# Four late matrix blocks of a decoder layer: another order of the sums, of the loads and of two products

## The chip, the core and the metric

The kernel runs on one core of one Trainium2 chip. TensorE (PE) multiplies matrices into PSUM, VectorE (DVE), ScalarE (ACT) and GpSimd (POOL) work element by element, and 16 DMA engines move data between HBM and SBUF. DMAs are issued from the queues of SyncE (SP), ScalarE and GpSimd. Each engine executes its own instructions in program order and waits on semaphores for the others. The metric is the device time of one execution in microseconds; the time of a kernel is the median of its runs.

## What is computed

The reference is one layer of a hybrid decoder over 512 tokens of width 2048 in float32. The part that the change touches is its end:

```python
merged = g_a * (o_a @ w_up_a[l]) + g_b * (o_b @ w_up_b[l])
x = x + merged @ w_out[l]
x = x + jax.nn.sigmoid(x @ w_ple_gate[l]) * (p[l] @ w_ple[l])
return rms_norm(x, final_g)
```

`w_out` and `w_ple_gate` are 2048 x 2048. What comes before (the projection of 2048 to 10800 columns, sparse attention, the gated spatial mixer and the two products up to `merged`) is the same in both kernels.

## The kernel before

**Accuracy.** A float32 operand is split into a high part, rounded by a cast on ScalarE (`high`, line 180), and a low part, the difference, on VectorE (`low`, line 186). Each product is then three matmuls (lines 443 to 445): high by high, high activations by low weights, low activations by high weights.

**Seven products instead of eight.** Each of the two matrix products at the end is done in a scheme of the Strassen kind. The 512 tokens are cut in two halves of 256 (two token tiles of 128 each), the 2048 contracted rows in two halves of 1024, and the 2048 columns in blocks. There are four such jobs, called the late blocks, in this order: `wo0` and `wo1` (for `w_out`), then `pg1` and `pg0` (for `w_ple_gate`). A block makes 1024 output columns, 512 of the left and 512 of the right half of the matrix, in seven products, named 1, 5, 6, 3, 7, 2 and 4. Each product has four pieces, 0 to 3, of 256 rows, so a block has 28 pieces; a piece is 12 matmuls of 128 x 512. Pieces are written as product and number: 70 is the first piece of product 7. The order is that of `LATE` (line 79): for wo0 and pg1

`10 11 12 13 20 21 50 51 22 23 52 53 60 30 61 31 62 32 63 33 70 71 72 73 40 41 42 43`

and for wo1 and pg0 the same with 52 53 before 22 23, and 60 61 62 63 before 30 31 32 33. "Piece 19" or "step 19" of a block below is the place in this order, counted from 0: in all four, places 20 to 23 are product 7 and places 24 to 27 product 4.

**PSUM.** A block has three pairs of banks (`BANK_OF`): products 1, 6, 7 and 4 accumulate one upon the other in the first pair, 5 and 3 in the second, 2 in the third. So each result has to be read out (`evac_late`) before the next product of the same pair starts. In `evac_late` products 1, 5 and 6 are copied by ScalarE (line 924); 3, 7 and 2 are combined on VectorE with an earlier copy straight out of PSUM (lines 930 and 932); 4 is the last.

**Weights of a block.** The first and second halves of the rows and of the columns give quarters 11, 12, 21 and 22, each in four tiles of 256 rows x 512 columns (512 KB). Operands of products are made in place: product 1 uses 11, 5 uses 11 + 12, 6 uses 11 + 12 + 22, 4 uses 11 + 12 + 22 + 21; product 2 uses 21, 3 uses 22, 7 uses 22 + 12. A sum is made either by a DMA that accumulates into the tile, issued by GpSimd (`add_later`, line 345), or on VectorE from a loaded tile (line 327, in `sum_to`). `adds` says which: "6" in `adds` means that 22 is accumulated by DMA for the first two pieces of product 6, "4" that 21 is accumulated by DMA for product 4. Without "4" the tiles of 21 are loaded a second time ("21b") and added on VectorE. The addition of 12 is always a DMA. Before the change wo0 and pg1 have "6", wo1 and pg0 have "4".

**Loads.** All loads of weights are issued by SP in the order of the list `loads` (`load_next`, `load_to`, line 291). Tiles of 11 have four places ("more"), all others five ("late": three named raw and two named ext). A load is put into the program once the last piece that read its place has been split; `held_till` puts a load later: not before the given piece has been split.

**Order of the instructions.** `gemm` writes the program piece by piece. At each step it first runs what was put off (`flush`, list `deferred`; `later` puts off by two steps), then `split_to`: the cast and the low part of the piece two further on, with sums, `add_later` and loads; then what `plan` and `plan_steps` have put at this step; then the 12 matmuls; after the last piece of a product its read-out. The buffers of high and low parts (`hs`, `ls`) have three places each, so a cast can be at most two pieces ahead of TensorE. An engine that waits on one of these instructions holds up all that were written after it for the same engine.

**Activations.** The operands of the next block's products are made beside the running block: eight transposes into two banks (`turn_pair`, line 2026), then sums on VectorE and casts on ScalarE (`first_half`, `second_half`). They are four sets, A, B, C and E, each a list of steps (A0, A1, ...), and a text in `plan_steps` says at which step of the block which of them stand. In `second_half`, 0 is the transposes with the high parts, 1 the first sum and low parts, and then follow casts of sums (ScalarE), their low parts and further sums (VectorE).

**End of a block.** Results of wo0 and wo1 are added to tiles of x (`add_x`, line 917), which `load_x` brings on ScalarE's queue. Those of pg1 and pg0 go through a tanh (`gate_x2`, line 956) and two operations of VectorE (949, 951). In pg0 product 4 is done token tile by token tile, and `finish_tile` scales and stores finished rows.

The loop over the token tiles in a piece, before:

```python
for i in range(2):
    k = 2 * j + i
    for t in range(2):
        o = sets[b][t]
        # three matmuls into o
if k == half - 1:
    job.evac(p, sets[b])
```

Of the kernel before, what the change touches and what calls it, by code (L numbers as in the profile page):

```python
# [102 lines left out]
def kernel(ctx: ExitStack, tc: tile.TileContext, x, p, norm_g, w_in,  # L103
                      pe_k, w1_k, w2_k, pe_v, w1_v, w2_v, ln_g, ln_b, sgu_w, sgu_b,
                      w_up_a, w_up_b, w_out, w_ple, w_ple_gate, final_g, out):
    nc = tc.nc
# [114 lines left out]
    def add_job(job):  # L221
        jobs.append(job)
        if job.kind == "S":
            half, c2 = job.kt // 2, job.c2
            ld = {}
            if job.grown:
# [120 lines left out]
    def split_to(i, more=1):  # L347
# [17 lines left out]
        while state["low"] <= min(i, len(subs) - 1):  # L365
# [16 lines left out]
            if job.grown and k == "7" and "4" in job.adds:  # L382
                add_later(job.grown, raw[ld["11", n]], "21", n)
# [11 lines left out]
    def gemm():  # L395
        si = 0
        for job in jobs:
            if job.kind == "S":
# [3 lines left out]
                for at, (p, j) in enumerate(products(job)):  # L402
# [33 lines left out]
                    for i in range(2):  # L436
                        k = 2 * j + i
                        st, sp = k == 0 and p in "152", k == half - 1
                        for t in range(2):
                            o = sets[b][t]  # L440
                            ah, al = job.act(p, k, t)
                            go = p not in "152"
                            nc.tensor.matmul(o, ah, hi[:, i], start=st, stop=False, skip_group_check=go)  # L443
                            nc.tensor.matmul(o, ah, lo[:, i], start=False, stop=False, skip_group_check=go)  # L444
                            nc.tensor.matmul(o, al, hi[:, i], start=False, stop=sp, skip_group_check=go)  # L445
                            if not (i and t):
                                yield
                    if k == half - 1:
                        job.evac(p, sets[b])
# [469 lines left out]
    def evac_late(i, final, fourth):  # L919

        def e(p, ps, t=None):
# [3 lines left out]
            elif p in "372":  # L925
                other, row, cg = {"3": ("6", 0, i + 2), "7": ("5", 2, i + 2), "2": ("1", 0, i)}[p]
# [15 lines left out]
    def final_wo(p, cg, row):  # L942
        other = {"3": "6", "7": "5", "2": "1"}[p]
        for t in range(2):
            if p != "2":
                later(partial(add_x, cg, row + t, kept[other][t]))
# [21 lines left out]
    def final_pg(p, cg, row):  # L968
        other = {"3": "6", "7": "5", "2": "1"}[p]
        for t in range(2):  # L970
# [1234 lines left out]
    plan_steps((late_jobs["wo0"], late_jobs["wo1"]), 0, "A0 A1B0 B1A2 C0A3 C1E0B2 E1B3 C2A4 C3E2A5 A6 E3A7 A8B4 B5C4 B6B7 B8C5 C6C7 C8E4 E5E6E7 E8", items)  # L2205
# [16 lines left out]
    plan_steps((late_jobs["wo1"], late_jobs["pg1"]), 9, "A0 A1 A2 A3B0 B1 B2 B3 C0 C1 C2E0 C3E1 E2 E3", items)  # L2222
    plan("wo1", 11, partial(load_x, 3, partial(new_gates, "x_3")))
    plan("wo1", 16, partial(load_x, 1, new_x))
# [87 lines left out]
```

## Time and profile before

| | |
|---|---|
| median of 3 runs | 1552.41 us (1551.02 to 1553.17) |
| profiled execution | 1551.73 us, span 1550.0 us |
| granted TensorE clock, mean | 0.989 |
| TensorE matmuls, busy | 1510.6 us (97%) |
| VectorE, busy | 1228.9 us (79%) |
| ScalarE, busy | 861.2 us (56%) |
| GpSimd, busy | 349.1 us (23%) |
| HBM read and written | 246.79 MB and 73.27 MB |

Busy time of TensorE counts modelled ends of pipelined matmuls, so gaps are read from the starts. A row of a timeline is: start, duration, engine, line, operation, what it writes and reads, shape, count; in brackets the idle time of the engine before it and what ended that. A row of waits is: engine, tile, line, what it waited for, then microseconds in total, times and the longest. A row of windows is: the stretch, its length, busy time and count of TensorE's matmuls, its weight loads, VectorE, ScalarE and GpSimd, then the granted clock, the share of the DMA engines and GB/s. A row "DMA tile<-source" of the chain is the time from issue to landing on which the chain waited; a row of DMA issues is queue, operation, count, size and the median time from issue to landing.

### The profile page before, as it was taken

What the parts mean: (1) busy time and instruction counts of PE and PEld (TensorE: products, weight loads), DVE (VectorE), ACT (ScalarE), POOL (GpSimd) and SP (SyncE); (2) the same over time, 40 slices, a digit from 0 to 9 for tenths busy, and PEclk for the clock granted to TensorE, in tenths of its full rate; (3) what the DMA queues carried; (4) which work ended last, traced back from release to release, by engine and by line L of the source; (5) the groups of instructions that cost most, each with busy time, mean ns of one, the idle gap of its engine ahead of it and who ended that gap; (6) DMA issues with size and microseconds to landing.
All of it is one profiled execution on the core that took longest, in us unless ns stands there. A gap on an engine that the chain in (4) does not pass through costs nothing.

```text
span 1550.0 us, 20203 instructions
## 1 busy us (share of the span) xinstructions
PE 1510.6 (97%) x7174; PEld 1255.2 (81%) x7174; DVE 1228.9 (79%) x1798; ACT 861.2 (56%) x1431; POOL 349.1 (23%) x495
## 2 busy tenths in 40 slices
PE   9999999999999999999999999999999999999995
PEld 8988888888888888888888888887888777777774
DVE  7787877777889787878588898859989976688576
ACT  6454455444555555555577776755556434455446
POOL 2232334220121111113214333321122110211120
PEclk9999999999999999999999999999999999999997
DMA  9897969582548585779634454377898776985875
GB/s 323 217 305 187 259 110 287 162 252 89 198 148 254 176 265 180 228 252 287 148 85 108 106 111 106 88 276 251 276 241 205 163 203 178 212 195 122 231 195 157
DMA packets 197076, 303.56 MB, mean 196 GB/s; under 512 B 30264, under 2 KB 91360, under 8 KB 195568
## 3 DMA queue, kind: packets, MB, share of 16 engines
q0 software_dynamic: 77856, 120.98, 33.6%
q1 hardware_dynamic: 104912, 149.57, 30.4%
q10 hardware_dynamic: 14208, 31.72, 6.0%
q8 instruction: 56, 0.92, 0.2%
q14 instruction: 44, 0.36, 0.1%
HBM read 246.79 MB, written 73.27 MB: 206 GB/s over the span
## 4 chain that ended last, share of the span: by engine, by line
PE 82%; DVE 6%; DMA 4%; ACT 4%; issue 3%; POOL 1%; ACTq 0%; DVEq 0%; POOLq 0%
PE ps_m L445 7%; PE ps_m L443 7%; PE ps_m L444 7%; DMA more<-in_w_out_dram 2%; DVE ls L186 2%; PE ps_pg L444 2%; PE ps_t L1710 2%; PE ps_pg L445 2%; PE ps_pg L443 2%; PE ps_za L474 2%; PE ps_za L473 2%; PE ps_za L472 2%; PE ps_u L443 2%; PE ps_kv L443 2%; PE ps_zb L443 2%
## 5 line engine op out<-in xcount | busy, mean ns | idle before, releaser
L186 DVE TENSOR_TENSOR ls<-b,hs 128x1024 fp32r<-128x1024 f32 x160 | 195.7, 1223 | 100.9 <-ACT hs L180 100.1
L180 ACT CAST hs<-b 128x1024 fp32r<-128x1024 f32 x160 | 168.1, 1052 | 189.9 <-PE ps_m L445 64.2
L180 ACT CAST hs<-raw 128x1024 fp32r<-128x1024 f32 x118 | 124.2, 1053 | 135.1 <-PE ps_m L445 28.9
L186 DVE TENSOR_TENSOR ls<-raw,hs 128x1024 fp32r<-128x1024 f32 x118 | 144.1, 1222 | 48.9 <-ACT hs L180 48.9
L180 ACT CAST hs<-more 128x1024 fp32r<-128x1024 f32 x95 | 99.9, 1052 | 117.8 <-DVE more L327 21.7
L186 DVE TENSOR_TENSOR ls<-more,hs 128x1024 fp32r<-128x1024 f32 x95 | 115.9, 1221 | 59.1 <-ACT hs L180 58.7
L443 PE MATMUL ps_m<-hs,act_h 128*128 128x512 f32 x256 | 100.2, 391 | 0.0
L445 PE MATMUL ps_m<-hs,act_l 128*128 128x512 f32 x256 | 99.6, 389 | 0.0
L444 PE MATMUL ps_m<-ls,act_h 128*128 128x512 f32 x256 | 99.6, 389 | 0.0
L186 DVE TENSOR_TENSOR lo<-raw,hi 128x512 fp32r<-128x512 f32 (+1 forms) x96 | 63.9, 670 | 19.9 <-PE ps_za L474 7.6
L332 DVE TENSOR_TENSOR b<-b,b 128x1024 f32<-128x1024 f32 x64 | 78.0, 1219 | 0.1
L332 DVE TENSOR_TENSOR b<-raw,b 128x1024 f32<-128x1024 f32 x64 | 77.9, 1218 | 0.0
L1659 ACT ACTIVATE prob<-prob,st 128x512 f32<-128x512 f32 (+3 forms) x128 | 70.8, 560 | 5.7 <-DVE st L1650 5.7
L1650 DVE CUSTOM_DVE_ANT_0 prob<-ps_s,b 128x512 f32<-128x512 f32 (+3 forms) x128 | 56.3, 486 | 13.7 <-PE ps_s L1646 13.5
L180 ACT CAST pth<-ps_t 128x512 fp32r<-128x512 f32 (+1 forms) x88 | 44.1, 547 | 35.0 <-PE ps_t L1710 34.5
L180 ACT CAST hi<-raw 128x512 fp32r<-128x512 f32 (+1 forms) x94 | 54.2, 588 | 15.9 <-PE ps_kw L473 4.0
L445 PEld LDWEIGHTS ps_m<-hs,act_l 128*128 128x128 f32 x256 | 48.1, 188 | 10.0
L444 PEld LDWEIGHTS ps_m<-ls,act_h 128*128 128x128 f32 x256 | 48.1, 188 | 9.8
L443 PEld LDWEIGHTS ps_m<-hs,act_h 128*128 128x128 f32 x256 | 48.1, 188 | 9.8
L186 DVE TENSOR_TENSOR ptl<-ps_t,pth 128x512 fp32r<-128x512 f32 (+1 forms) x88 | 52.4, 633 | 3.4 <-ACT pth L180 3.4
L443 PE MATMUL ps_wo<-hs,m_h 128*128 128x512 f32 x128 | 51.1, 399 | 2.3 <-DVE keep L932 1.3
L444 PE MATMUL ps_wo<-ls,m_h 128*128 128x512 f32 x128 | 50.8, 397 | 1.8 <-DVE ls L186 1.8
(661 smaller groups left out, 4566.3 us busy)
## 6 DMA issues: line engine op xcount, KB each, us to landing
raw<-in_w_in_dram SPq DMA_DIRECT2D x100, 512.0 KB, 4.4
b<-in_w_in_dram SPq DMA_DIRECT2D x64, 512.0 KB, 5.8
more<-in_w_out_dram POOLq DMA_DIRECT2D x14, 512.0 KB, 10.6
more<-in_w_ple_gate_dram POOLq DMA_DIRECT2D x14, 512.0 KB, 11.5
gate<-keep ACTq DMA_DIRECT2D x24, 256.0 KB, 6.4
raw<-in_w_up_b_dram SPq DMA_DIRECT2D x12, 512.0 KB, 7.4
raw<-in_w_up_a_dram SPq DMA_DIRECT2D x12, 512.0 KB, 5.6
raw<-in_w_out_dram SPq DMA_DIRECT2D x12, 512.0 KB, 9.9
```

Of the source, the lines that this page charges most:

```text
L180: nc.scalar.copy(hi, src)
L186: nc.vector.tensor_tensor(out=lo, in0=src, in1=hi.bitcast(F32), op=ALU.subtract)
L332: nc.vector.tensor_tensor(out=b[o], in0=b[x], in1=b[y], op=ALU.subtract)
L443: nc.tensor.matmul(o, ah, hi[:, i], start=st, stop=False, skip_group_check=go)
L444: nc.tensor.matmul(o, ah, lo[:, i], start=False, stop=False, skip_group_check=go)
L445: nc.tensor.matmul(o, al, hi[:, i], start=False, stop=sp, skip_group_check=go)
L472: nc.tensor.matmul(ps, hi[:, j], ah, start=st, stop=False)
L473: nc.tensor.matmul(ps, hi[:, j], al, start=False, stop=False)
L474: nc.tensor.matmul(ps, lo[:, j], ah, start=False, stop=sp)
L1650: nc.vector.tensor_tensor_reduce(out=pt[:, j * n:j * n + n], in0=o[:, j], in1=b0[:, 512 - n:], scale=-SLOPE[h], scalar=3.0e38, op0=ALU.add ...
L1659: nc.scalar.activation(sl, sl, AF.Exp, bias=st[:, 0, j, hh:hh + 1], scale=-1.0, accum_out=st[:, 1, j, hh:hh + 1])
L1710: nc.tensor.transpose(b[:, (2 * e + hh) * P:(2 * e + hh + 1) * P], pts[hh][:, c:c + P], ident)
```

## The change

It does six things, all in the late blocks:

- Products 7 and 4 do their pieces token tile by token tile: the six matmuls of tile 0, then the six of tile 1. Product 7 is read out per token tile: ScalarE copies it to `kept["6"]` as soon as that tile's last matmul has been written into the program, half-way through piece 73 for tile 0, and the subtraction on VectorE is put off to the next step.
- The texts of `plan_steps` place casts of sums on ScalarE one step after the sum on VectorE that they read, and the low part in the step of its cast; most steps of sets stand earlier than before. B in pg1 turns into bank "t" instead of "s".
- `adds` is "64" for wo0, "4" for wo1, "64" for pg1 and nothing for pg0. So wo0 and pg1 accumulate 21 by DMA, and pg0 loads 21b and adds on VectorE.
- Before each DMA that accumulates 21, GpSimd copies one element of the tile of 22, so that it waits for what was accumulated into that tile.
- The load of the third tile of 21 is held in the program until piece 3 of its block has been split.
- `load_x`, `add_x`, `load_x2` and `load_fg` (the broadcast of `final_g`, 1 MB) stand at other steps.

```diff
@@ add_job
                 if first:
                     held_till.update({ld["21", 3]: len(subs) + 4, ld["22", 0]: len(subs) + 7})
+                held_till[ld["21", 2]] = len(subs) + 3
@@ split_to
             if job.grown and k == "7" and "4" in job.adds:
+                nc.gpsimd.tensor_copy(small[0:1, 76:77], raw[ld["22", n]][0:1, 0, 0:1])
                 add_later(job.grown, raw[ld["11", n]], "21", n)
@@ gemm
-                    for i in range(2):
+                    turned = job.grown and p in "74"
+                    for n in range(4):
+                        t, i = divmod(n, 2) if turned else (n % 2, n // 2)
...
+                        if turned and sp and p == "7":
+                            job.evac(p, sets[b], t)
+                        if n < 3:
+                            yield
-                    if k == half - 1:
+                    if k == half - 1 and not (turned and p == "7"):
                         job.evac(p, sets[b])
@@ evac_late
+            elif p == "7":
+                nc.scalar.copy(kept["6"][t], ps[t])
+
+                def difference(o=kept["5"][t], x=kept["6"][t], t=t):
+                    nc.vector.scalar_tensor_tensor(out=o, in0=x, scalar=-1.0, in1=o, op0=ALU.mult, op1=ALU.subtract)
+                    final(p, i + 2, 2, (t,))
+                deferred.append(difference)
@@ final_wo
-                later(partial(add_x, cg, row + t, kept[other][t]))
+                (deferred.append if p == "7" else later)(partial(add_x, cg, row + t, kept[other][t]))
@@ final_pg
-                (deferred.append if cg % 2 == 0 else later)(f)
+                (deferred.append if cg % 2 == 0 or p == "7" else later)(f)
@@ late_jobs
-                                       seq=LATE[at], adds="64"[at])
+                                       seq=LATE[at], adds={"wo0": "64", "wo1": "4", "pg1": "64", "pg0": ""}[f"{n}{i}"])
@@ plans, wo0
-"A0 A1B0 B1A2 C0A3 C1E0B2 E1B3 C2A4 C3E2A5 A6 E3A7 A8B4 B5C4 B6B7 B8C5 C6C7 C8E4 E5E6E7 E8"
+"A0 A1B0 B1A2A3 C0B2B3 C1E0 E1C2C3 E2E3A4 A5A6 A7A8B4 B5B6 B7B8C4 C5C6 C7C8E4 E5E6 E7E8"
-    plan("wo0", 19, partial(load_x, 0, new_x))
-    for n, at in (("wo0", 24), ("wo1", 25)):
+    plan("wo0", 21, partial(load_x, 0, new_x))
+    for n, at in (("wo0", 26), ("wo1", 26)):
@@ plans, wo1 from step 9
-"A0 A1 A2 A3B0 B1 B2 B3 C0 C1 C2E0 C3E1 E2 E3"
-    plan("wo1", 11, partial(load_x, 3, partial(new_gates, "x_3")))
-    plan("wo1", 16, partial(load_x, 1, new_x))
+"A0 A1 A2A3 B0 B1 B2B3 - C0 C1 C2C3E0 E1 E2E3"
+    plan("wo1", 14, partial(load_x, 3, partial(new_gates, "x_3")))
+    plan("wo1", 21, partial(load_x, 1, new_x))
@@ plans, wo1 from step 25 and pg1 (banks of A, B, C, E first)
-("gg", "ss", "gg", "oo")
-"A0 A1B0 B1A2 A3 A4B2 B3C0 B4C1E0 E1 A5C2 C3E2A6 E3A7B5 B6 B7 C4 C5C6 C7 C8 E4 E5E6 E7 E8"
+("gg", "tt", "gg", "oo")
+"A0 A1B0 B1A2 A3A4 B2 C0B3B4 C1E0A5 E1C2C3 E2E3A6A7 C4B5 C5C6B6B7 C7C8 E4 E5E6 E7E8"
@@ plans, pg0
-    plan("pg0", 9, partial(load_x2, 0, "h2"))
-    plan("pg0", 11, partial(load_x2, 2, "h1"))
+    plan("pg0", 8, partial(load_x2, 0, "h2"))
+    plan("pg0", 10, partial(load_x2, 2, "h1"))
-    plan("pg0", 15, load_fg)
+    plan("pg0", 14, load_fg)
```

More of the change, by code (lines that the diff above doesn't have):

```diff
@@ L435, in gemm @@
                         sets[b] = [bank(job.banks[b], f"ps_{job.name}{b}{t}") for t in range(2)]
-                    for i in range(2):
+                    turned = job.grown and p in "74"
+                    for n in range(4):
+                        t, i = divmod(n, 2) if turned else (n % 2, n // 2)
                         k = 2 * j + i
                         st, sp = k == 0 and p in "152", k == half - 1
[L439 to L447, printed above, removed]
-                    if k == half - 1:
+                        o = sets[b][t]
+                        ah, al = job.act(p, k, t)
+                        go = p not in "152"
+                        nc.tensor.matmul(o, ah, hi[:, i], start=st, stop=False, skip_group_check=go)
+                        nc.tensor.matmul(o, ah, lo[:, i], start=False, stop=False, skip_group_check=go)
+                        nc.tensor.matmul(o, al, hi[:, i], start=False, stop=sp, skip_group_check=go)
+                        if turned and sp and p == "7":
[3 more added lines that the diff above has]
+                    if k == half - 1 and not (turned and p == "7"):
                         job.evac(p, sets[b])
@@ L924, in e @@
                     nc.scalar.copy(kept[p][t], ps[t])
-            elif p in "372":
-                other, row, cg = {"3": ("6", 0, i + 2), "7": ("5", 2, i + 2), "2": ("1", 0, i)}[p]
+            elif p == "7":
[4 more added lines that the diff above has]
+                deferred.append(difference)
+            elif p in "32":
+                other, row, cg = {"3": ("6", 0, i + 2), "2": ("1", 0, i)}[p]
                 for t in range(2):
@@ L940, in evac_late, with final_wo @@
         return e
-    def final_wo(p, cg, row):
+    def final_wo(p, cg, row, ts=(0, 1)):
         other = {"3": "6", "7": "5", "2": "1"}[p]
-        for t in range(2):
+        for t in ts:
             if p != "2":
-                later(partial(add_x, cg, row + t, kept[other][t]))
+                (deferred.append if p == "7" else later)(partial(add_x, cg, row + t, kept[other][t]))
     def ple_add(cg, t, sg, piece):
@@ L966, in gate_x2, with final_pg @@
         (deferred.append if soon else later)(second)
-    def final_pg(p, cg, row):
+    def final_pg(p, cg, row, ts=(0, 1)):
         other = {"3": "6", "7": "5", "2": "1"}[p]
-        for t in range(2):
+        for t in ts:
             o = kept[other][t]
@@ L2204 @@
     plan("wo0", 5, lambda: sums_at.update(x=new_x()))
-    plan_steps((late_jobs["wo0"], late_jobs["wo1"]), 0, "A0 A1B0 B1A2 C0A3 C1E0B2 E1B3 C2A4 C3E2A5 A6 E3A7 A8B4 B5C4 B6B7 B8C5 C6C7 C8E4 E5E6E7 E8", items)
+    plan_steps((late_jobs["wo0"], late_jobs["wo1"]), 0, "A0 A1B0 B1A2A3 C0B2B3 C1E0 E1C2C3 E2E3A4 A5A6 A7A8B4 B5B6 B7B8C4 C5C6 C7C8E4 E5E6 E7E8", items)
     plan("wo0", 8, partial(load_x, 2, partial(new_gates, "x_2")))
-    plan("wo0", 19, partial(load_x, 0, new_x))
-    for n, at in (("wo0", 24), ("wo1", 25)):
+    plan("wo0", 21, partial(load_x, 0, new_x))
+    for n, at in (("wo0", 26), ("wo1", 26)):
         for t in range(2):
@@ L2221 @@
                                  partial(sums_tile, *third), ("gg", "gg", "gg", "tt")[n])
-    plan_steps((late_jobs["wo1"], late_jobs["pg1"]), 9, "A0 A1 A2 A3B0 B1 B2 B3 C0 C1 C2E0 C3E1 E2 E3", items)
-    plan("wo1", 11, partial(load_x, 3, partial(new_gates, "x_3")))
-    plan("wo1", 16, partial(load_x, 1, new_x))
+    plan_steps((late_jobs["wo1"], late_jobs["pg1"]), 9, "A0 A1 A2A3 B0 B1 B2B3 - C0 C1 C2C3E0 E1 E2E3", items)
+    plan("wo1", 14, partial(load_x, 3, partial(new_gates, "x_3")))
+    plan("wo1", 21, partial(load_x, 1, new_x))
     def second_places():
@@ L2240 @@
         items[name] = second_half(embedded, q, lambda cg=cg: x_tiles[cg], j, partial(sums_tile, *own),
-                                  partial(sums_tile, "6", 2), a21 and partial(sums_tile, *a21), ("gg", "ss", "gg", "oo")[n])
+                                  partial(sums_tile, "6", 2), a21 and partial(sums_tile, *a21), ("gg", "tt", "gg", "oo")[n])
     plan("wo1", 23, second_places)
     plan("pg1", 2, more_places)
-    plan_steps((late_jobs["wo1"], late_jobs["pg1"]), 25, "A0 A1B0 B1A2 A3 A4B2 B3C0 B4C1E0 E1 A5C2 C3E2A6 E3A7B5 "
-               "B6 B7 C4 C5C6 C7 C8 E4 E5E6 E7 E8", items)
+    plan_steps((late_jobs["wo1"], late_jobs["pg1"]), 25, "A0 A1B0 B1A2 A3A4 B2 C0B3B4 C1E0A5 E1C2C3 "
+               "E2E3A6A7 C4B5 C5C6B6B7 C7C8 E4 E5E6 E7E8", items)
     plan("pg1", 2, lambda: x2_tiles.update({1: x_tiles[1], 3: x_tiles[3]}))
```

## The prediction

> **What bounds the kernel now.** I read the page first (span, chain), then TensorE's matmuls in order of time around the four late blocks, then who ended TensorE's waits there, then VectorE's and the DMA engines' load.
>
> ```profile
> span 1550.0 us, 20203 instructions
> PE 82%; DVE 6%; DMA 4%; ACT 4%; issue 3%; POOL 1%; ACTq 0%; DVEq 0%; POOLq 0%
> ```
>
> The chain that ends last is TensorE's, and the diff touches only the last quarter. The blocks begin here (in this order wo0, wo1, pg1, pg0), and the last matmul is the sixth row. The seventh, from the chain, is one turn of eight transposes:
>
> ```profile
> 1183.32 0.48 PE L443 MATMUL ps_wo<-hs,m_h 128*128 128x512 f32 x1
> ...
> 1271.16 0.39 PE L443 MATMUL ps_wo<-hs,m_h 128*128 128x512 f32 x1
> 1271.38 0.39 PE L444 MATMUL ps_wo<-ls,m_h 128*128 128x512 f32 x1
> ...
> 1360.64 0.47 PE L443 MATMUL ps_pg<-hs,ob_h 128*128 128x512 f32 x1 [1.87 <-DVE s L186]
> ...
> 1448.76 0.39 PE L443 MATMUL ps_pg<-hs,ob_h 128*128 128x512 f32 x1
> ...
> 1536.38 0.39 PE L420 MATMUL ps_pg<-ob_h,m_l 128*128 128x512 f32 x1
> 1307.34 0.87 PE ps_m L2026 x8
> ```
>
> Undisturbed matmuls start 0.227 us apart, so a block of 28 pieces x 12 is 76.3 us and a piece 2.72. Less that and its transposes (0.9 for each turn inside it: three, six, two, none), wo0 (87.8 us) lost 8.8, wo1 (89.5) 7.7, pg1 (88.1) 10.0 and pg0 (88.0 to the end of its last matmul) 11.7: **38 us lost in all**. The change can win no more there. The losses of single pieces below are counted the same way, between their first matmuls. Who ended these waits:
>
> ```profile
> PE ps_pg L443 <- DVE keep L932: 4.9, 1, 4.9
> PE ps_wo L444 <- DVE ls L186: 4.9, 7, 1.0
> PE ps_pg L418 <- DVE keep L932: 3.5, 1, 3.5
> PE ps_pg L443 <- DVE s L186: 1.9, 1, 1.9
> PE ps_wo L443 <- DVE keep L932: 1.3, 2, 0.8
> ```
>
> L932 is the seventh product read out of PSUM, for which the fourth waits in the same bank; L186 is the low half of a weight piece. The rest is matmuls at half clock after such a wait, one row of it below.
>
> **The change part by part.**
>
> *Seventh product.* In pg1 its two read-outs stand on VectorE behind sums (L327) and low halves of later pieces:
>
> ```profile
> 1434.96 1.28 DVE L932 SCALAR_TENSOR_TENSOR keep<-ps_pg,keep 128x512 f32<-128x512 f32 x2
> 1435.79 0.77 PE L443 MATMUL ps_pg<-hs,s 128*128 128x512 f32 x1 [4.92 <-DVE keep L932]
> ```
>
> ```profile
> L924 ACT COPY keep<-ps_pg 128x512 f32<-128x512 f32 x12 | 7.0, 586 | 5.1 <-PE ps_pg L445 4.4 <-DVE x L186 0.2
> ```
>
> Now ScalarE copies a tile (0.59), issued half-way through piece 23 for token tile 0 (1.36 us before the piece ends), behind only the cast of piece 25. So copy 0 ends before piece 24, and copy 1 (0.6 after piece 23) within piece 24's first 1.36. What is late next is that cast: it waits for the accumulating DMA. A quiet one takes 6.3 us, as the row of 1396 to 1426 says; the last of four issued behind one another landed after 14.3:
>
> ```profile
> raw<-in_w_ple_gate_dram POOLq DMA_DIRECT2D x3, 512.0 KB, 6.3
> ...
> 1333.20 14.32 DMA more<-in_w_out_dram
> ```
>
> The four took 33.3% of 34 us of the DMA engines in the row of 1264 to 1298 below, 2.8 apiece; so the second "21" lands some 12 us after the low half of piece 19, 15 after piece 17's start, while the copy's end is wanted 19 after that start. Hidden, with 3 to spare after the cast. The subtraction moves to VectorE's next piece at the same 0.68. Won: in pg1 4.9 + 0.2 and 2.1 of half clock, 7.2, of which I take 6.9; in wo0 1.2, in wo1 0.6 (both in the items below).
>
> *wo0, pieces 22 to 24, 5.0 us.* The third copy of "22" lands late under three plain loads of "21b" beside it:
>
> ```profile
> 1241.65 10.85 DMA raw<-in_w_out_dram
> ```
>
> "4" among the additions removes these loads and four 1.14 us sums (in pg1 too), and puts four accumulations behind it. At 6.3 it lands before its cast is due. Gain 4.9 with the 1.2 above. The POOL copy of one element costs only its wait for "22"; behind it stand only later "21". Bound: nothing if the pieces come at 10.9 again, 5.0.
>
> *wo0, pieces 15 to 19, 3.9 us: VectorE is the limit.*
>
> ```profile
> 1193.00:1242.00 49.00, 47.13 (x207) 37.17 (x205) 44.66 (x61) 26.75 (x36) 6.32 (x6) 1.00 0.73 165
> ```
>
> Its 4.3 idle microseconds (3.8 of them waits for ScalarE) are all that the new order can take. I count the queue: the rows below give 0.67 for two of 256 columns, 1.19 for two of 512, 1.14 for a low half.
>
> ```profile
> 1190.28 0.75 DVE L2033 SCALAR_TENSOR_TENSOR keep<-ps_m,a 128x256 f32<-128x256 f32 x2
> 1190.95 1.28 DVE L188 SCALAR_TENSOR_TENSOR m_l<-ps_m,m_h 128x512 fp32r<-128x512 f32 x2
> 1192.14 1.21 DVE L186 TENSOR_TENSOR ls<-raw,hs 128x1024 fp32r<-128x1024 f32 x1
> ```
>
> A set (A, B, C or E) is 1.9 + 0.6 + 1.3 + 1.9 + 0.6 = 6.3 (a dependent pair 1.3 instead of 1.2). From 1192.14 to the end of piece 17's low half stand 14 low halves (16.0), A without its first part and three sets (23.5), two sums and two read-outs (3.5): 43.0, with 0.3 of waiting to 1235.4. TensorE undisturbed wants it at 1232.6. So 2.9 us stay of 3.9: the work is done sooner, but it also stands ahead of low halves sooner. Gain 1.0 (bounds -1 and 3.9).
>
> *wo1, pieces 8 and 9, 2.4 us:* casts wait for accumulations of the operand "12".
>
> ```profile
> 1276.68 19.97 DMA more<-in_w_out_dram
> ...
> q0 software_dynamic: 1088, 2.10, 33.3%
> q10 hardware_dynamic: 1056, 2.10, 16.0%
> ```
>
> ```profile
> 1266.94 0.42 SPq L291 DMA_DIRECT2D raw<-in_w_out_dram  x1
> 1267.42 0.97 SPq L291 DMA_DIRECT2D ext<-in_w_out_dram  x2
> 1268.49 11.02 SPq L291 DMA_DIRECT2D raw<-in_w_out_dram  x3
> ```
>
> The first five leave SP in a row because their places are free (the last row's third came 11 us later). Holding "21", 2 back moves its place in the program, but SP has only these loads in its queue, in the same order, and gets no new wait. I take the hold as nothing (bounds 0 and 2.4).
>
> *wo1, pieces 19 to 24, 3.3 us.* load_x of tile 1 stood before the transposes that still read its place, and ScalarE's casts stood behind it:
>
> ```profile
> 1326.36 0.92 ACTq L2165 DMA_DIRECT2D x<-in_x_dram  x2
> 1327.32 1.05 ACT L180 CAST hs<-ext 128x1024 fp32r<-128x1024 f32 x1 [5.19 <-PE ps_m L2026]
> ```
>
> At piece 21 those have run; its landing (5 to 6 us) is wanted at 26. Gain 2.8: 0.5 stays, since the turn at piece 25 needs the seventh's additions, which stand behind low half 26 and so behind a "21".
>
> *Begin of pg1 and its pieces 17 to 19, 5.0 us* (2.0 at 1360.64, 1.7 of half clock, 1.3). B's turned pair leaves bank "s" (pg1's first) for "t" (first needed at piece 4), so that wait goes. But VectorE is next:
>
> ```profile
> 1352.00:1379.00 27.00, 25.13 (x116) 20.54 (x116) 22.52 (x34) 14.64 (x21) 5.44 (x5) 0.94 0.93 233
> ```
>
> From wo1's piece 26 to pg1's low half 13 its queue holds 14 low halves (16.0), A and B (7.0 each), C and E (12.0), four additions (2.4), two read-outs (1.2): 45.6 against 15 pieces and three turns, 43.4. So 2.2 stay, gain 2.8 (bounds 0 and 5.0).
>
> *pg0* gives up "4": four loads and four 1.14 us sums return, where VectorE has no gap:
>
> ```profile
> 1515.24 1.22 DVE L186 TENSOR_TENSOR ls<-ext,hs 128x1024 fp32r<-128x1024 f32 x1
> ...
> 1517.58 2.35 DVE L186 TENSOR_TENSOR ls<-more,hs 128x1024 fp32r<-128x1024 f32 x2
> 1519.85 0.15 DVE L988 TENSOR_REDUCE small<-small 128x1 f32<-128x4 f32 x1
> ...
> 1521.99 1.28 DVE L932 SCALAR_TENSOR_TENSOR keep<-ps_pg,keep 128x512 f32<-128x512 f32 x2
> ```
>
> Three sums, 3.4 us, come ahead of L988. load_fg one piece earlier clears the way for "22", and low half 22 starts about 2.8 us sooner; L988 is then 0.6 later. ScalarE's copies of the seventh stand behind finish_tile(0), whose scalings end 0.6 later than their 1523.2, so the copy ends at 1524.4 where the first L932 ended at 1522.7:
>
> ```profile
> 1521.85 1.32 ACT L1004 ACTIVATE x<-x,small 128x512 f32<-128x512 f32 x2
> ...
> 1522.82 0.76 PE L418 MATMUL ps_pg<-hs,s 128*128 128x512 f32 x1 [3.50 <-DVE keep L932]
> 1523.38 0.63 PE L419 MATMUL ps_pg<-ls,s 128*128 128x512 f32 x1
> ```
>
> The fourth starts 1.5 later, the end, which ScalarE and VectorE carry from here, 1.2 later. Cost 1.2 (bounds: 4.3 if the "22" land no sooner, a gain of 3 if VectorE keeps up).
>
> *The rest at nothing.* Matmuls of products seven and four in the other order of token tiles are the same 12 to a piece with the same low half, which the piece has to have two matmuls in either way. load_x of tiles 3 and 0, add_x and load_x2 move by one to five pieces with the same instructions and transfers; what hides them is that their data is used four pieces later or more, and a lost cover would cost one landing, 5 to 8 us, once. The rows of additions on VectorE (L917) two pieces later meet pieces without sums.
>
> **Sum:** 6.9 + 4.9 + 1.0 + 0 + 2.8 + 2.8 - 1.2 = 17.2 us. The profiled execution took 1551.73 (span 1550.0), the median of the runs is 1552.41, 0.7 above it; 1552.4 - 17.2 = **1535.2 us**.
>
> The Trainium skill (TensorE: Matmul & The Clock Gate, Part 1: The HAM clock gate) lets the clock fall only after an idle window of about 3.4 us. The trace differs: a wait of 1.87 us at 1360.64 goes with a clock of 0.94 over 27 us, 1.6 us. By the rule alone the half clock at wo0 and at pg1's begin (3 us) would not hang on these waits, and the sum would be 14; the row decides.
>
> **The rivals.**
>
> *VectorE binds more than I count* (0.19). For it: 91% busy in wo0's stretch; against it: its idle time there. The two gains under it fall to 0 (-3.8) and pg0 costs 4.3 (-3.1): 10.3 won, 1542.
>
> *The waits go nearly all* (0.18): the hold acts (2.4), VectorE loses nothing in pg1 (2.2), and pg0 gains 2 instead of its cost (3.2). 25 won, 1527. Against it: the SP rows, and VectorE's queue.
>
> *Nothing won* (0.03): what is won in wo0 and pg1 is lost again behind late sums in pg0.
>
> *Slower* (0.10): one mechanism, accumulations too late. An accumulation takes twice the DMA time of a plain transfer (33.3% against 16.0% for 2.10 MB), and casts of the fourth's pieces wait for it with the seventh's copies behind them on ScalarE. If the "21" land in wo0, wo1 and pg1 as the last did at 1276 (20 us), the copy comes 5 us late with 2 of half clock in each: 21 lost against 17.2 won, 1556. It decides from a landing of 16 us on; for it speaks that row, against it the quiet 6.3. The Trainium skill (DMA: Bandwidth & Descriptors, Issuing engines are not separate DMA queues) says that all queues share 16 engines, which those shares agree with.
>
> **How the numbers follow.** Forecast 0.50, its own range 1530 to 1541. With the rivals the range is 1525 to 1547: it leaves out the last two and half of the better one's far side. About 0.2% (3 us) is what can be told from no change: faster 0.87, same 0.03, slower 0.10.
>
> **What would show it.** wo0 about 82 us from first to next first matmul, wo1 with pg1's begin about 84.5, pg1 about 80.5; no wait for L932 from the fourth's first matmul outside pg0; pg1's begin without a wait for s; no 5 us gap of ScalarE before L2165. SP's five loads still in a row at wo1's begin, and pieces 8 and 9 still late. In pg0 the fourth begins later in the block than now. I am wrong in place if wo0 or pg1 keep over 4 us of waits for low halves, in sign if the casts of the fourth's pieces wait for "21".

## The result, and the profile after

The changed kernel takes 1540.2 us (median of 4 runs, 1538.6 to 1540.4) against 1552.8 us (1551.0 to 1553.4) on the same chip: a ratio of 0.9918 with an interval of 0.9901 to 0.9936. It is faster by 12.6 us. The prediction was 1535.2 us, so 5.0 us are missing. The experiments show that its two largest terms can be won by other edits too than those it named, and that the cost in pg0 was put too low.

The page of the changed kernel has this span and this chain, and TensorE's timeline these first matmuls of the blocks and this last one:

```profile
span 1538.5 us, 20227 instructions
PE 83%; DVE 8%; ACT 3%; DMA 3%; issue 2%; POOL 0%; DVEq 0%; ACTq 0%; POOLq 0%
```

```profile
1183.55 0.48 PE L446 MATMUL ps_wo<-hs,m_h 128*128 128x512 f32 x1
...
1265.74 0.39 PE L446 MATMUL ps_wo<-hs,m_h 128*128 128x512 f32 x1
...
1351.45 0.39 PE L446 MATMUL ps_pg<-hs,ob_h 128*128 128x512 f32 x1
...
1433.21 0.39 PE L446 MATMUL ps_pg<-hs,ob_h 128*128 128x512 f32 x1
...
1524.50 0.39 PE L422 MATMUL ps_pg<-ob_h,m_l 128*128 128x512 f32 x1
```

The span is 11.5 us shorter. wo0 now takes 82.2 us (before 87.8), wo1 85.7 (89.5) and pg1 81.8 (88.1): 15.8 won. From the begin of pg0 to the end of the span it is 105.3 instead of 101.2: 4.1 lost. (The remaining 0.2 is the later begin of wo0.)

TensorE's three largest waits in the four blocks of the changed kernel, in total, times and the longest:

```profile
PE ps_pg L420 <- ACT keep L931: 5.1, 1, 5.1
PE ps_pg L447 <- DVE ls L186: 5.0, 4, 3.1
PE ps_wo L447 <- DVE ls L186: 2.9, 4, 1.2
```

The waits of 4.9 and 1.3 us for the seventh product (L932) and of 1.9 for bank "s" are gone. The first row is the seventh product again, now ScalarE's copy (L931), and it stands once, in pg0. In the list cut to pg1 alone no row names the seventh product.

The following table, worked out from each trace in the same way (first matmul of a block to that of the next, the last column from pg0's first matmul to the end of the span), carries the experiments. The kernels were timed on several chips, on which the kernel before took 1552.8 to 1554.1 us; each ratio is to the kernel before on the same chip, and medians some 1 us apart in different rows may differ by the chip alone:

| kernel | median, us | ratio to before (interval) | wo0 | wo1 | pg1 | pg0 and end |
|---|---|---|---|---|---|---|
| before | 1552.8 | | 87.8 | 89.5 | 88.1 | 101.2 |
| changed | 1540.2 | 0.9918 (0.9901 to 0.9936) | 82.2 | 85.7 | 81.8 | 105.3 |
| pg0_four | 1535.0 | 0.9884 (0.9869 to 0.9899) | 82.1 | 85.7 | 81.7 | 99.8 |
| finish_later | 1539.6 | 0.9915 (0.9900 to 0.9930) | 82.4 | 85.4 | 82.0 | 104.1 |
| no_four | 1541.5 | 0.9926 (0.9912 to 0.9941) | 82.1 | 85.8 | 83.6 | 105.7 |
| seventh_old | 1540.4 | 0.9917 (0.9900 to 0.9933) | 82.8 | 84.9 | 83.6 | 104.4 |
| both_back | 1544.8 | 0.9944 (0.9929 to 0.9959) | 82.8 | 85.9 | 87.3 | 103.5 |
| order_only | 1547.1 | 0.9967 (0.9955 to 0.9979) | 82.8 | 86.5 | 89.2 | 103.5 |
| old_order | 1544.1 | 0.9941 (0.9926 to 0.9956) | 85.2 | 88.5 | 80.3 | 104.5 |
| old_far_loads | 1542.4 | 0.9930 (0.9914 to 0.9945) | 83.6 | 87.4 | 81.7 | 104.8 |
| no_hold | 1538.8 | 0.9916 (0.9901 to 0.9931) | 82.2 | 85.1 | 81.8 | 105.0 |
| held_by_queue | 1531.9 | 0.9860 (0.9843 to 0.9876) | 82.1 | 83.1 | 81.9 | 99.5 |
| finish_25 | 1531.9 | 0.9872 (0.9855 to 0.9888) | 82.2 | 83.3 | 81.9 | 99.0 |
| finish_25_order | 1534.0 | 0.9883 (0.9868 to 0.9897) | 82.1 | 82.8 | 82.1 | 102.1 |

### The profile page after: what moved, and what is told of

It is laid out like the page before. It is cut to its first block, busy times and chain, and to the rows that moved or that the text cites. A ratio compares the mean times of both kernels' runs of the same rounds, so it can differ in the third digit from the quotient of the medians.

```text
span 1538.5 us, 20227 instructions
## 1 busy us (share of the span) xinstructions
PE 1502.8 (98%) x7174; PEld 1251.8 (81%) x7174; DVE 1225.2 (80%) x1794; ACT 865.2 (56%) x1439; POOL 355.6 (23%) x511
## 4 chain that ended last, share of the span: by engine, by line
PE 83%; DVE 8%; ACT 3%; DMA 3%; issue 2%; POOL 0%; DVEq 0%; ACTq 0%; POOLq 0%
PE ps_m L446 7%; PE ps_m L447 7%; PE ps_m L448 7%; DVE ls L186 2%; PE ps_wo L447 2%; PE ps_wo L448 2%; PE ps_wo L446 2%; PE ps_t L1722 2%; PE ps_za L479 2%; PE ps_za L478 2%; PE ps_za L477 2%; PE ps_u L446 2%; PE ps_zb L446 2%; PE ps_kv L446 2%; PE ps_vn L446 2%
## 5 line engine op out<-in xcount | busy, mean ns | idle before, releaser
L180 ACT CAST hs<-more 128x1024 fp32r<-128x1024 f32 x95 | 99.8, 1052 | 108.4 <-DVE more L328 26.7
L477 PE MATMUL ps_za<-act_h,hi 128*128 128x512 f32 x128 | 52.4, 409 | 0.0
L477 PE MATMUL ps_q<-act_h,hi 128*128 128x512 f32 x128 | 52.2, 407 | 0.0
## 6 DMA issues: line engine op xcount, KB each, us to landing
more<-in_w_out_dram POOLq DMA_DIRECT2D x18, 512.0 KB, 10.9
```

The source lines that it names most:

```text
L180: nc.scalar.copy(hi, src)
L477: nc.tensor.matmul(ps, hi[:, j], ah, start=st, stop=False)
```

## The experiments

### What pg0 loses

In pg0 of the changed kernel VectorE's timeline shows three of the four sums (L328) ahead of the sum of squares of token tile 0 (L1000):

```profile
1499.92 1.22 DVE L328 TENSOR_TENSOR more<-more,raw 128x1024 f32<-128x1024 f32 x1
1501.06 1.22 DVE L186 TENSOR_TENSOR ls<-raw,hs 128x1024 fp32r<-128x1024 f32 x1
...
1503.39 1.22 DVE L328 TENSOR_TENSOR more<-more,ext 128x1024 f32<-128x1024 f32 x1
1504.53 1.22 DVE L186 TENSOR_TENSOR ls<-more,hs 128x1024 fp32r<-128x1024 f32 x1
1505.66 1.22 DVE L328 TENSOR_TENSOR more<-more,ext 128x1024 f32<-128x1024 f32 x1
1506.80 1.22 DVE L186 TENSOR_TENSOR ls<-more,hs 128x1024 fp32r<-128x1024 f32 x1
1507.93 0.16 DVE L1000 TENSOR_REDUCE small<-small 128x1 f32<-128x4 f32 x1
```

ScalarE waits for it with a loaded table, then scales token tile 0, and only then makes the copies for which TensorE waits (ScalarE's timeline, and TensorE's row):

```profile
1505.79 1.28 ACT L1006 ACT_TABLE_LOAD   x1
1508.31 0.20 ACT L1006 ACTIVATE small<-small 128x1 f32<-128x1 f32 x1 [1.24 <-DVE small L1001]
...
1509.94 1.32 ACT L1016 ACTIVATE x<-x,small 128x512 f32<-128x512 f32 x2
1511.16 1.05 ACT L931 COPY keep<-ps_pg 128x512 f32<-128x512 f32 x2
```

```profile
1511.77 0.79 PE L420 MATMUL ps_pg<-hs,s 128*128 128x512 f32 x1 [5.12 <-ACT keep L931]
```

Two kernels ask whether the sums or the place of the copies cost the time. The first:

```diff
-adds={"wo0": "64", "wo1": "4", "pg1": "64", "pg0": ""}[f"{n}{i}"])
+adds={"wo0": "64", "wo1": "4", "pg1": "64", "pg0": "4"}[f"{n}{i}"])
```

> The changed kernel with one thing put back: block pg0 keeps "4" among its additions, so POOL adds the second terms of its fourth product by DMA and VectorE makes none of the four sums (L328). Theory V: pg0's loss is VectorE's queue. Three sums of 1.14 us stand ahead of the sum of squares of token tile 0 (L1000 at 1507.93), on which ScalarE and the seventh product's copies hang, so without them the wait of TensorE ahead of the fourth product falls from 5.1 us to 2 or less and the time to about 1536 (1535 to 1537.5). Theory P, the price of the prediction: giving up "4" cost 1.2 us, so about 1539 (1538.5 to 1539.5), and the rest of pg0's loss stands in the place of the copies behind token tile 0's scalings on ScalarE.

1535.0 us: theory V. Putting back this one string wins 5.2 us, and pg0 with the end takes 99.8 us, 1.4 less than in the kernel before. But the wait for the copies fell only to 3.2 us, not to 2 or less. The second:

```diff
-    plan("pg0", 23, partial(finish_tile, 0))
+    plan("pg0", 24, partial(finish_tile, 0))
```

> The changed kernel with finish_tile(0) of pg0 planned at piece 24 instead of 23, so that ScalarE has the two copies of the seventh product ahead of the table load, the root and the scalings of token tile 0. Theory S: the copies' place on ScalarE is the link that holds the fourth product. They then end right behind piece 23, the fourth begins 3 to 4 us sooner in the block, and the time is about 1537 (1536 to 1538.5). Theory E: from piece 23 on the end hangs on the sum of ScalarE's and VectorE's work and not on its order; the fourth begins sooner but its later pieces wait instead, and the time stays at 1540 (1539.3 to 1541).

1539.6 us: theory E. Fourth product and copies come sooner, as S says, and then TensorE waits further on. Its longer waits from the fourth product on, in the timeline of finish_later:

```profile
1504.78 0.50 PE L420 MATMUL ps_pg<-hs,s 128*128 128x512 f32 x1 [1.18 <-ACT keep L931]
1510.02 0.50 PE L421 MATMUL ps_pg<-ls,m_h 128*128 128x512 f32 x1 [1.81 <-DVE ls L186]
1514.18 0.79 PE L420 MATMUL ps_pg<-ob_h,m_h 128*128 128x512 f32 x1 [2.74 <-ACT ob_h L180]
```

The fourth begins at 1504.78 instead of 1511.77, and the last matmul ends at 1524.2 instead of 1524.9.

### The seventh product's read-out and the sums of the fourth

Undone one by one:

```diff
-adds={"wo0": "64", "wo1": "4", "pg1": "64", "pg0": ""}[f"{n}{i}"])
+adds={"wo0": "6", "wo1": "4", "pg1": "6", "pg0": ""}[f"{n}{i}"])
```

> The changed kernel with "4" taken out of the additions of wo0 and pg1 (pg0 has none as it is): the four plain loads and four sums of VectorE come back in both blocks. Theory P, the prediction: in wo0 the third copy of "22" comes late again under these loads and piece 22 and 23 lose 3.7 us, in pg1 the sums delay low halves by up to 1.1 each; 1540.2 + 4 to 6 = about 1545 (1544 to 1547). Theory N: the seventh product's own read-out was what held the blocks, and with it on ScalarE the sums lie in VectorE's gaps: 1540 to 1542.

1541.5 us: theory N, wo0 unchanged, pg1 1.8 us longer.

```diff
-turned = job.grown and p in "74"
+turned = job.grown and p == "4"
...
-            elif p == "7":
-                nc.scalar.copy(kept["6"][t], ps[t])
...
-            elif p in "32":
-                other, row, cg = {"3": ("6", 0, i + 2), "2": ("1", 0, i)}[p]
+            elif p in "372":
+                other, row, cg = {"3": ("6", 0, i + 2), "7": ("5", 2, i + 2), "2": ("1", 0, i)}[p]
```

> The changed kernel with the seventh product as it was: its pieces go through both token tiles in turn, and VectorE reads both halves out of PSUM after the last piece (the fourth product keeps its new order). Theory P, the prediction: these read-outs stand behind low halves on VectorE and TensorE waits in each block, 6.9 + 1.2 + 0.6 us less what the missing sums now spare VectorE in pg1: about 1547 (1545 to 1549). Theory N: with the sums of the fourth's operand gone VectorE reads the two halves at once, and a block loses only the two read-outs of 0.6 and the latency, 1.5 us: about 1544 (1542 to 1545).

1540.4 us: both theories priced it too high. Without the new read-out pg1 loses 1.8 us and wo0 0.6; wo1 is 0.8 and pg0 with the end 0.9 shorter. The edit that was to win 6.9 us can be taken out at no cost in the time. The two together:

> The changed kernel with both edits to the fourth and seventh product put back at once: no "4" among the additions of wo0 and pg1, and the seventh product read out by VectorE after its last piece. Each alone cost 1.3 and 0.2 us. Theory A, they add: the first three blocks lose 3 to 4 us and pg0 wins 1, about 1542.5 (1541.5 to 1543.5). Theory C, each covers for the other: with sums and read-outs both on VectorE the stalls of the kernel before come back in wo0 (4.9) and pg1 (7.1): about 1550 (1547 to 1552).

1544.8 us, and neither theory whole: pg1 loses 5.5 us (theory C), wo0 0.6 (theory A). The wait for the seventh product in the list of waits from 1400 to 1440, first of seventh_old, then of both_back:

```profile
PE ps_pg L446 <- DVE keep L937: 1.6, 1, 1.6
```

```profile
PE ps_pg L446 <- DVE keep L937: 3.7, 1, 3.7
```

In pg1 it took VectorE's sums and VectorE's read-outs together to make the long wait; each edit alone removes most of what pg1 loses (3.7 of 5.5 us).

### What won wo0's pieces 22 to 24

In both_back wo0 has "21b" loaded and summed as before, and still does not lose the 5.0 us of these pieces. Three edits could have done it: the order of the sums, the far loads, "4". The last kernel of this group is both_back with the far loads put back:

```diff
-    plan("wo0", 21, partial(load_x, 0, new_x))
+    plan("wo0", 19, partial(load_x, 0, new_x))
-    plan("wo1", 14, partial(load_x, 3, partial(new_gates, "x_3")))
-    plan("wo1", 21, partial(load_x, 1, new_x))
+    plan("wo1", 11, partial(load_x, 3, partial(new_gates, "x_3")))
+    plan("wo1", 16, partial(load_x, 1, new_x))
```

> The kernel both_back (1544.8 us) with the loads of the far tiles put back too, so that of the change only the new order of the operand sums with bank "t", the hold on SP and pg0 without "4" are left. Question: what won the 5.0 us of wo0's pieces 22 to 24. Theory P, the prediction: "4" among the additions, which takes three plain loads away from the third copy of "22"; without it that copy lands some 10 us after its issue again, wo0 loses 8 us in all against 3.7 in both_back, and with 1.7 in wo1 the time is about 1551 (1549.5 to 1552.5). Theory O: the new order is enough, because the copy is issued 3 us sooner (1238.5 against 1241.65) and the loads come after it; wo0 stays at 4 to 5 us and the time is 1547 (1546 to 1548.5).

1547.1 us: theory O. Its rows on GpSimd's and SP's queue and of its DMA issues show the third copy of "22":

```profile
1238.33 1.19 POOL L346 DMA_DIRECT2D raw<-in_w_out_dram  x1 [1.22 <-DVE ls L186]
```

```profile
1240.83 0.37 SPq L292 DMA_DIRECT2D ext<-in_w_out_dram  x1
```

```profile
raw<-in_w_out_dram POOLq DMA_DIRECT2D x1, 512.0 KB, 6.9
```

It lands after 6.9 us instead of 10.9, with the same plain loads and the same far tile behind it. It is issued 3.3 us sooner than in the kernel before, because the low half that frees its tile is made sooner, and so it has a start of 2.5 us on the first load. Of the three edits asked about, the order of the sums is enough here (the places of `add_x` and the fourth product's order of token tiles are still those of the change).

### The order, and the far loads, undone alone

```diff
-    plan_steps((late_jobs["wo0"], late_jobs["wo1"]), 0, "A0 A1B0 B1A2A3 C0B2B3 C1E0 E1C2C3 E2E3A4 A5A6 A7A8B4 B5B6 ...
+    plan_steps((late_jobs["wo0"], late_jobs["wo1"]), 0, "A0 A1B0 B1A2 C0A3 C1E0B2 E1B3 C2A4 C3E2A5 A6 E3A7 A8B4 B5C4 ...
...
-                                  ... ("gg", "tt", "gg", "oo")[n])
+                                  ... ("gg", "ss", "gg", "oo")[n])
```

(The other two texts likewise.)

> The changed kernel with the order of the operand sums as it was: the three texts that plan_steps lays out in wo0, wo1 and pg1, and bank "s" for B's turned pair; additions, seventh product and late loads stay changed. Theory P, the prediction's prices: 1.0 in wo0 and 2.8 with pg1's begin come back, 1540.2 + 3.8 = 1544 (1543 to 1546). Theory O: the order of the sums is the main part, because putting back "no four" or the old seventh product alone cost next to nothing in wo0 and 1.8 us in pg1; then the losses of wo0's pieces 17 to 23 and of pg1's pieces 17 to 24 come back with it, some 9 us: 1549 (1547 to 1551).

1544.1 us: theory P, in sum. In the blocks: 3.0 us come back in wo0 and 2.8 in wo1, while pg1 is 1.5 shorter with the old text. Bank "s" makes pg1's first matmul wait again, 3.1 us (its row stands in the last section).

But of the 5.0 us of wo0's pieces 22 to 24 only 0.9 come back with the old order. The third copy of "22", by GpSimd's row of old_order and its landing, is issued as late as before the change, and lands in 6.1 us instead of 10.9:

```profile
1241.66 1.18 POOL L346 DMA_DIRECT2D raw<-in_w_out_dram  x1 [6.65 <-DVE ls L186]
raw<-in_w_out_dram POOLq DMA_DIRECT2D x1, 512.0 KB, 6.1
```

The three plain loads are gone here, by "4", and the load of the far tile is issued at 1247.89 instead of 1242.11; which of the two does more was not tried apart. So these pieces too can be won in two ways, by the order or by a quiet copy.

The far loads alone (the diff above, nothing else):

> The changed kernel with the loads of the far tiles where they were: tile 0 at piece 19 of wo0 instead of 21, tile 3 at 11 of wo1 instead of 14, tile 1 at 16 of wo1 instead of 21. Theory P, the prediction's price: only tile 1 matters, its issue holds up ScalarE's casts behind the transposes of wo1, 2.8 us: 1543 (1542 to 1544). Theory L: tile 0's 1 MB at piece 19 of wo0 also shares the DMA engines with the additions by DMA that piece 22 waits for, so that wo0 loses 3 to 4 us more: 1546.5 (1545 to 1548). Theory N: with the new order the transposes are earlier and nothing waits: 1540 to 1541.

1542.4 us, 2.2 back, nearest to theory P; but half of it is L's. 1.7 us are lost in wo1, and 1.5 in wo0, where tile 0's load at piece 19 stands beside the additions of "21". The DMA issues between 1239.3 and 1246.5, of the changed kernel and then of old_far_loads:

```profile
more<-in_w_out_dram POOLq DMA_DIRECT2D x4, 512.0 KB, 11.1
```

```profile
more<-in_w_out_dram POOLq DMA_DIRECT2D x4, 512.0 KB, 14.0
x<-in_x_dram ACTq DMA_DIRECT2D x2, 512.0 KB, 12.0
```

### The hold on SP, and what pieces 7 to 9 of wo1 wait for

```diff
-                held_till[ld["21", 2]] = len(subs) + 3
```

> The changed kernel without its one line that holds "21" 2 back. Theory P, the prediction: SP has nothing but these loads in its queue, in the same order, so that the line moves no transfer: 1540.2 (1539.5 to 1541), pieces 7 to 9 of wo1 lose 2.9 us as before. Rival: the hold delays the loads where a wait of SP lies between, and without it wo1's pieces 6 to 9 lose more: 1541.5 to 1543.

1538.8 us (1538.6 to 1539.6): the line moves nothing that can be measured. SP's queue of the changed kernel still sends its five loads in a row, the first of each row below at 1262.55 and 1263.59; without the line they start at 1262.81 and 1263.86:

```profile
1262.55 0.93 SPq L292 DMA_DIRECT2D ext<-in_w_out_dram  x2
1263.59 2.38 SPq L292 DMA_DIRECT2D raw<-in_w_out_dram  x3
```

A hold that works puts them behind an instruction that waits. On pg0_four:

```diff
-            nc.sync.dma_start(t, src)
+            (nc.scalar if state["loads"] in by_act else nc.sync).dma_start(t, src)
...
+                if job.name == "wo1":
+                    held_till[ld["21", 2]] = len(subs) + 5
+                    by_act.update({ld["21", 2], ld["21", 3], ld["22", 0]})
...
-    plan("wo0", 27, partial(store_x2, 2))
-    plan("wo1", 2, partial(store_x2, 0))
+    plan("wo1", 8, partial(store_x2, 2))
+    plan("wo1", 10, partial(store_x2, 0))
```

> The kernel pg0_four (1535.0 us), and in wo1 three plain loads ("21" 2 and 3, "22" 0) issued on ScalarE's queue behind its cast of piece 6, where SP sends them at once; and the stores of tiles 2 and 0 moved from wo0's piece 27 and wo1's 2 to wo1's 8 and 10. Theory H: pieces 7 to 9 of wo1 lose 2.9 us because the additions by DMA for pieces 6 to 9 share the DMA engines with these 1.5 MB and 2 MB; with both moved the additions land within 9 us, pieces 7 to 9 lose nothing, and the time is 1532 (1531.3 to 1533). Theory Q: the additions are slow by themselves, 2.7 us apiece one behind another and issued 2.7 apart, and land as late without neighbours: no change, 1535 (1534.3 to 1536).

1531.9 us: theory H. wo1 is 2.6 us shorter and its pieces 7 to 9 lose nothing. The DMA issues between 1263 and 1272, of the changed kernel and then of held_by_queue:

```profile
x_d<-x ACTq DMA_DIRECT2D x2, 1024.0 KB, 17.8
more<-in_w_out_dram POOLq DMA_DIRECT2D x4, 512.0 KB, 16.8
raw<-in_w_out_dram SPq DMA_DIRECT2D x3, 512.0 KB, 18.5
```

```profile
more<-in_w_out_dram POOLq DMA_DIRECT2D x4, 512.0 KB, 9.7
```

The same four additions land in 9.7 us instead of 16.8 once 1.5 MB of loads and 2 MB of stores are elsewhere. Which of the two moves does more was not tried apart. That transfers from three queues slow one another agrees with the Trainium skill (DMA: Bandwidth & Descriptors, Issuing engines are not separate DMA queues), by which all queues use the same 16 engines. This kernel beats both: 1.4% below the one before, where the change is 0.8% below it.

### Can TensorE's loss in pg0 be won?

On held_by_queue, with the sums gone, the last two kernels move the finishing of token tiles 0 and 1 behind all casts of the fourth's pieces:

```diff
-    plan("pg0", 23, partial(finish_tile, 0))
-    plan("pg0", 25, partial(finish_tile, 1))
+    plan("pg0", 25, partial(finish_tile, 0))
+    plan("pg0", 26, partial(finish_tile, 1))
```

> The kernel held_by_queue (1531.9 us) with token tile 0 of pg0 finished at step 25 instead of 23, so behind the copies of the seventh product and all casts of the fourth's pieces, and token tile 1 at step 26. Theory S: with the sums gone from VectorE only the place of the copies on ScalarE holds the fourth product back (4.8 us, and 2.6 at half clock); 1528.5 (1527 to 1530). Theory E: as in finish_later, the work of ScalarE and VectorE from there to the end sets the time in any order: 1531.9 (1531 to 1533).

1531.9 us, the same median (on another chip; the ratios to the kernel before are 0.9872 and 0.9860): nothing is won, as theory E has it. TensorE's last matmul of held_by_queue, then of finish_25:

```profile
1518.39 0.39 PE L425 MATMUL ps_pg<-ob_h,m_l 128*128 128x512 f32 x1
```

```profile
1510.63 0.39 PE L425 MATMUL ps_pg<-ob_h,m_l 128*128 128x512 f32 x1
```

TensorE is done 7.8 us sooner and nothing of it reaches the end. In the chain of waits of finish_25 the last transfer lands at 1501.76, and from there on no piece is TensorE's, up to the output:

```profile
1491.81 9.95 DMA more<-in_w_ple_gate_dram
...
1501.78 1.05 ACT ob_h L180
1502.83 1.05 ACT keep L971 x2
1503.90 1.28 ACT L1009
```

So it is not only the work of ScalarE and VectorE that sets the end here: the finishing of token tile 0 now stands behind a cast that waits for an accumulation by DMA.

With the third text of plan_steps (pg1's sums) as before the change, bank "t" kept:

```diff
-    ... 25, "A0 A1B0 B1A2 A3A4 B2 C0B3B4 C1E0A5 E1C2C3 "
-               "E2E3A6A7 C4B5 C5C6B6B7 C7C8 E4 E5E6 E7E8", items)
+    ... 25, "A0 A1B0 B1A2 A3 A4B2 B3C0 B4C1E0 E1 A5C2 C3E2A6 E3A7B5 "
+               "B6 B7 C4 C5C6 C7 C8 E4 E5E6 E7E8", items)
```

> The kernel finish_25 with the third text of plan_steps (the sums of pg1) as it was before the change, and bank "t" kept. Theory B: the bank alone removed the wait at pg1's begin, and the new text itself costs pg1 the 2 us at its pieces 5 and 10, where old_order loses nothing: 1.5 us faster than finish_25, with 0.6 to 2 lost at pieces 17 to 23. Theory V: VectorE has no room with the old text either; the same time as finish_25 within 0.7 us, or slower where the seventh product's end meets late sums.

1534.0 us: not theory B. pg1 takes 82.1 us against 81.9, so once bank "t" is there the texts differ by nothing in pg1; old_order's short pg1 came after a begin that had waited 3.1 us; whether that is why is only argued. Why the end of pg0 came out 3 us longer in its trace stays open.

## Why the prediction was right or wrong, step by step

| where | predicted gain | measured | what of it failed |
|---|---|---|---|
| wo0 | 5.9 | 5.6 | size right, the cause one of two |
| wo1 with pg1's begin | 5.0 | 3.8 | additions under loads, a turn |
| pg1 | 7.6 | 6.4 | size nearly, cause half |
| pg0 and end | -1.2 | -4.1 | a sum mis-sized, wrong limit |

(Predicted by block: 87.8 to 82, 89.5 to 84.5, 88.1 to 80.5.) By the traces, 2.9 us of what is missing are pg0's and 2.7 lie in the first three blocks.

*The bound.* That TensorE's waits in these blocks set the time held for wo0, wo1 and pg1: what their traces lose or win, the time loses or wins. For pg0 it was false. The 11.7 us counted there as TensorE's were counted as winnable, but finish_25 took 7.8 of them and won nothing. The chain of the kernel before said so already, read to its end and not by its shares: its last piece of TensorE stands at 1508.91, in pg0's piece 21, and all behind it, up to the last output at 1545.5, is ScalarE's, VectorE's or an issue:

```profile
1508.91 0.24 PE ps_pg L445
1509.18 1.03 ACT hs L180
...
1545.11 0.40 DVE x L1006
```


*pg0, "the fourth starts 1.5 later, the end 1.2 later".* The failed step is "load_fg one piece earlier clears the way for 22, and low half 22 starts about 2.8 us sooner". VectorE's rows of the low half of piece 22, before and after:

```profile
1510.24 1.23 DVE L186 TENSOR_TENSOR ls<-ext,hs 128x1024 fp32r<-128x1024 f32 x1 [1.63 <-ACT hs L180]
```

```profile
1494.91 1.23 DVE L186 TENSOR_TENSOR ls<-raw,hs 128x1024 fp32r<-128x1024 f32 x1 [1.63 <-ACT hs L180]
```

Measured from the block's first matmul, it starts 0.2 us later, 61.7 instead of 61.5. The row at 1515.24 in the prediction is the low half of piece 23: it starts 1.4 later (1501.06 after, 67.9 instead of 66.5), because the first of the three sums stands ahead of it. With all three sums, 3.4 us, the sum of squares comes 3.6 later (74.7 instead of 71.1), not 0.6. The copies of "22" land no sooner. For the third, GpSimd's rows of before and after and their landing:

```profile
1497.18 1.20 POOL L345 DMA_DIRECT2D ext<-in_w_ple_gate_dram  x1 [2.13 <-DVE ls L186]
ext<-in_w_ple_gate_dram POOLq DMA_DIRECT2D x1, 512.0 KB, 10.5
```

```profile
1482.07 1.21 POOL L346 DMA_DIRECT2D raw<-in_w_ple_gate_dram  x1 [2.12 <-DVE ls L186]
raw<-in_w_ple_gate_dram POOLq DMA_DIRECT2D x1, 512.0 KB, 10.1
```

It lands 58.9 us into the block in both. The cast that waits for the second copy starts no sooner either, at 55.1 us (1503.89) and 55.4 (1488.57). The rest of the step held: the fourth starts 4.5 us later instead of 1.5 and the end 4.1 instead of 1.2, both about 3 more, as much as the 2.8 that did not come. The prediction had named this case as its bound ("4.3 if the 22 land no sooner"), and 4.1 was measured; the step chose the wrong end of its own range. pg0_four prices "4" at 5.2 us in the median; there the low half of piece 22 starts 60.9 us into the block, 0.8 sooner than with the four loads of "21b".

*Seventh product, 6.9 us.* The mechanism was read rightly (the read-outs stood behind sums and low halves), and the "21" landed in time: in wo0 11.1 us after issue in the median of the row above, below the 16 from which the slower rival would have decided; no cast of the fourth's pieces is late in the three blocks. But the gain was given to the read-out alone. It belongs to either of two edits: without one or the other pg1 loses 1.8, without both 5.5. A wait behind a queue of several things is mostly gone once any one that is long enough is removed, so terms of one queue must not be priced one by one. (The rival's "twice the DMA time of a plain transfer" compares accumulations with stores; the loads of that stretch took 44.9% of the engines for 4.72 MB, so it is 1.7 times against loads.)

*wo0's pieces 22 to 24, 4.9 us by "4".* These pieces lose nothing now, so the size holds. The mechanism was right, but it was one of two: with the old order the copy lands in 6.1 us without the plain loads (old_order), where the prediction said 6.3, and 0.9 is lost. What the prediction did not see is that the new order issues the copy 3.3 us sooner and is enough too: order_only keeps the three plain loads and loses 0.6 there.

*wo0's pieces 15 to 19.* Right: "2.9 stay". Pieces 12, 15 and 16 lose 2.8, and VectorE is idle 0.7 us of 43, by the row of the changed kernel's windows (its busy time is the third):

```profile
1193.00:1236.00 43.00, 41.25 (x185) 32.70 (x184) 42.29 (x59) 24.71 (x34) 4.78 (x4) 1.00 0.72 165
```

*wo1.* The hold as nothing was right (no_hold), and pieces 8 and 9 are still late: with piece 7 they lose 2.9 (before 2.4). load_x(1) was right in kind: ScalarE's gap is gone, and old_far_loads brings it back at 1.7 us in wo1, against 2.8. What stays is 1.1 at the turn of piece 24, against 0.5.

*Tile 0's load "at nothing".* Wrong: at its old place it costs wo0 1.5 us (old_far_loads), because it then shares the DMA engines with the additions of "21", that the change itself had put there.

*pg1's begin.* The wait for "s" went, as said. "2.2 stay" was 3.3, and at other places: two turns, and pieces 5, 10 and 12 instead of 17 to 19.

*The order of the sums.* Priced at 3.8 (1.0 and 2.8), undone alone it costs 3.9. Without "4", the new read-out and the later far loads (order_only) it wins 6.9 us in the first three blocks: much of what it wins the other edits win as well.

## What to carry to other kernels

Price what stands in one queue together: when two edits remove parts of the same wait, neither term may be added to the other, and a kernel with both undone shows the sum. Before counting an engine's waits as winnable, ask whether the chain ends with that engine; in the last block here its 7.8 us were free. To hold a transfer back, put it behind an instruction that waits, since a later place in a queue that never waits moves nothing.

## What the hardware showed unexpectedly

The prediction took from a wait of 1.87 us with a granted clock of 0.64 behind it that such waits cost half clock. In old_order the same first matmul of pg1 waited 3.08 us at full clock. The windows from pg1's begin of before and of old_order (the clock is the third number from the end), and the latter's row:

```profile
1360.60:1364.00 3.40, 3.36 (x10) 2.69 (x11) 3.37 (x6) 0.62 (x1) 0.00 (x0) 0.64 1.05 208
```

```profile
1357.00:1362.00 5.00, 5.00 (x22) 4.12 (x23) 4.97 (x8) 2.20 (x3) 0.60 (x1) 1.00 1.07 235
```

```profile
1357.00 0.47 PE L446 MATMUL ps_pg<-hs,ob_h 128*128 128x512 f32 x1 [3.08 <-DVE s L186]
```

Over all the traces here, 15 waits of TensorE from 1.87 to 3.08 us in these blocks were followed by matmuls at half clock (0.43 us apart) in 11 cases and in four not (1.98 in finish_25 and in held_by_queue, 2.84 in finish_later, 3.08 in old_order); all 15 from 3.11 us on were. So half clock behind a wait of 2 to 3 us is no fixed price; what decides it was not tried. The Trainium skill (TensorE: Matmul & The Clock Gate, Part 1: The HAM clock gate) says that activity is watched in a free-running window of about 3.4 us; that the same wait comes with and without half clock agrees with it, that 1.87 us are enough does not agree with a whole window of idleness.
